# A second copy of x with its columns on partitions in place of the transposes of its rows, norm factors spread by a matrix product, and two alternating units in the first block

## The chip, the core and the metric

The kernel runs on one core of one Trainium2 chip. The metric is the device time of one execution in microseconds (us). A core has TensorE for matrix products (PE in the profile, its weight loads PEld), VectorE (DVE), ScalarE (ACT), GpSimd (POOL) and SyncE (SP), whose queue issues nearly all DMA transfers here. Each engine works through its own instructions in order and waits on the others by semaphores.

## What is computed

One layer of a streaming encoder over 4096 prompt frames and 64 sample frames with a model width of 1024, cut to what the change touches:

```python
def rms_norm(x, w):
    y = x * lax.rsqrt(jnp.mean(x * x, axis=-1, keepdims=True) + EPS)
    return y * w

h = rms_norm(x, norm_in_w) @ w_in          # 1024 -> 5648 columns
u, v, g, z, xbc, dt_raw = jnp.split(h, SPLITS, axis=-1)
# gMLP branch: s = u * (W_s LN(v) + b), times silu(g)
# SSD branch: conv + silu on xBC, scan over chunks with dt, times silu(z)
y = x + concat([a_out, b_out]) @ w_out     # then a last rms_norm
```

All values are float32. A product on TensorE contracts over partitions, so the normalised rows of x are needed with the 1024 columns of x on partitions, not with the frames there.

## The kernel before

**Blocks and stages.** The frames stand in chunks of 128. Five blocks of six chunks (768 frames) are worked through in turn by `Strassen(bi).run()`, and then a last block with two prompt chunks and the 64 sample frames. A block goes through the stages v, conv, u and g, and z; the z stage also builds the operands of the next block. After all blocks a second phase multiplies by w_out.

**Products.** The input projection of a block uses a scheme with seven products in place of eight (`ORDER = 1, 2, 4, 6, 7, 5, 3`). Each operand is split into a rounded part and a rest ("hi" and "lo"), and a product adds hi·hi, hi·lo and lo·hi. The operands that come from x are the tiles `hop[1]` to `hop[7]`, each with hi and lo; in rows of the trace they are all `hop`. They are made from `xq`, the normalised x with columns on partitions (a view of the tile `arena`), by the steps T1 to T4 (line 524, 527, 530, 533) and `split` (cast on ACT, line 514, and a subtraction, line 515). With frames cut in halves h = 0, 1 and columns in halves kh = 0, 1, `xq` has four quarters b11, b12 (kh = 0) and b21, b22 (kh = 1). `hop[1]` needs the quarter b11 alone and `hop[2]` the quarter b21 alone; all the others need the second half of the frames too.

**x before.** For the first block `rows0_load`, `rows0_norm` and `rows0_turn` load each chunk's rows, square and sum them on ACT, raise the mean to -1/2 on POOL (line 123), multiply the rows on DVE (line 612), transpose them on PE (line 619) and copy them out of PSUM with the factor `norm_in_w` (lines 624 and 626). For later blocks `xrows` does the same in the z stage (lines 479, 481, 488, 491), once for each half of the columns, so every chunk is loaded one and a half times.

**Weights.** In the first block the class `Operands` makes the weight operands from `w_in` (`make`): sums of raw tiles a11, a12, a21, a22 (tiles `wx`, `wa`), a cast on ACT (line 392) and a subtraction on DVE or POOL (line 393), and it stores them in DRAM (`wop_v` and others, line 397) for later blocks, which load them again (line 417, 420). A request of unit v takes two tiles `w` of four, so two products of v can be ready at a time, and a tile is free again when its product is done and its store has landed.

**Order of the work.** Filler steps are spread over the products by `fill.tick()`. In the v stage of the first block, `hooks` puts the making of `hop[3]` to `hop[7]` behind the first products of unit v0; unit v1 follows with the same seven operands. A scheduler in the language decides the final order on each engine's queue; the lists below show it.

## Time and profile before

| | |
|---|---|
| median of three runs | 2957.9 us (2953.92 to 2960.72) |
| the profiled execution | 2957.03 us, its span 2955.1 us |
| PE busy | 2826.3 us (96%) |
| DVE busy | 2162.7 us (73%) |
| ACT busy | 1345.8 us (46%) |
| POOL busy | 704.8 us (24%) |
| DMA | 679.14 MB, 230 GB/s in the mean |

The page is read from the top: PE is the busiest engine over the whole span, so a gain has to come from fewer columns streamed on PE, from less waiting of PE, or from a higher granted clock. The queries that follow cut the span by stage.

### The profile page before, as it was taken

What the parts mean: (1) busy time and instruction counts of PE and PEld (TensorE: products, weight loads), DVE (VectorE), ACT (ScalarE), POOL (GpSimd) and SP (SyncE); (2) the same over time, 40 slices, a digit from 0 to 9 for tenths busy, and PEclk for the clock granted to TensorE, in tenths of its full rate; (3) what the DMA queues carried; (4) which work ended last, traced back from release to release, by engine and by line L of the source; (5) the groups of instructions that cost most, each with busy time, mean ns of one, the idle gap of its engine ahead of it and who ended that gap; (6) DMA issues with size and microseconds to landing.
All of it is one profiled execution on the core that took longest, in us unless ns stands there. A gap on an engine that the chain in (4) does not pass through costs nothing. (4 is left out here: it accounts for less than half of the span.)

```text
span 2955.1 us, 46403 instructions
## 1 busy us (share of the span) xinstructions
PE 2826.3 (96%) x17159; PEld 2633.3 (89%) x17159; DVE 2162.7 (73%) x3607; ACT 1345.8 (46%) x2655; POOL 704.8 (24%) x575
## 2 busy tenths in 40 slices
PE   5988988999999999999999999999999899999998
PEld 5987887999999999999999999999899688878886
DVE  7888887667756777676677576874666766698887
ACT  4366655145643266541565514663365222253332
POOL 4554443110012100031000221000301433353332
PEclk8999998999999999999999999999999899999999
DMA  6666777777787777886777877778777555454553
GB/s 223 252 233 237 258 281 261 245 229 238 248 277 270 229 238 243 270 288 227 244 241 240 300 264 229 234 246 281 241 251 226 168 171 171 159 169 157 171 171 111
DMA packets 306809, 679.14 MB, mean 230 GB/s; under 512 B 30472, under 2 KB 154072, under 8 KB 306584
## 3 DMA queue, kind: packets, MB, share of 16 engines
q1 hardware_dynamic: 305544, 676.17, 68.6%
q8 instruction: 137, 2.24, 0.3%
q14 instruction: 88, 0.72, 0.1%
q10 hardware_dynamic: 1040, 0.00, 0.0%
HBM read 525.34 MB, written 150.75 MB: 229 GB/s over the span
## 5 line engine op out<-in xcount | busy, mean ns | idle before, releaser
L1123 PE MATMUL mm<-hop,w 128*128 128x384 f32 x1656 | 579.4, 350 | 7.1 <-ACT w L392 3.5
L1125 PE MATMUL mm<-hop,w 128*128 128x384 f32 x1656 | 564.9, 341 | 9.0 <-DVE w L393 4.5
L1124 PE MATMUL mm<-hop,w 128*128 128x384 f32 x1656 | 565.0, 341 | 0.0
L1629 PE MATMUL pa<-wlo,oh 128*128 128x512 f32 (+1 forms) x928 | 366.7, 395 | 13.0 <-DVE wlo L1583 13.0
L1630 PE MATMUL pa<-whi,ol 128*128 128x512 f32 (+1 forms) x928 | 364.9, 393 | 3.5 <-DVE ol L1591 3.5
L1628 PE MATMUL pa<-whi,oh 128*128 128x512 f32 (+1 forms) x928 | 365.2, 394 | 2.6 <-ACT whi L1582 1.4
L1123 PEld LDWEIGHTS mm<-hop,w 128*128 128x128 f32 x1656 | 315.4, 190 | 14.0 <-ACT w L392 7.0
L1125 PEld LDWEIGHTS mm<-hop,w 128*128 128x128 f32 x1656 | 315.3, 190 | 12.2 <-DVE w L393 7.0
L1124 PEld LDWEIGHTS mm<-hop,w 128*128 128x128 f32 x1656 | 315.5, 190 | 3.4 <-issue 2.4
L1123 PE MATMUL mm<-hop,wy 128*128 128x384 f32 x864 | 297.4, 344 | 0.0
L1125 PE MATMUL mm<-hop,wy 128*128 128x384 f32 x864 | 292.0, 338 | 0.0
L1124 PE MATMUL mm<-hop,wy 128*128 128x384 f32 x864 | 291.9, 338 | 0.0
L1629 PEld LDWEIGHTS pa<-wlo,oh 128*128 128x128 f32 (+1 forms) x928 | 174.6, 188 | 57.1 <-DVE wlo L1583 18.9
L1630 PEld LDWEIGHTS pa<-whi,ol 128*128 128x128 f32 (+1 forms) x928 | 174.8, 188 | 42.7 <-DVE ol L1591 4.2
L1628 PEld LDWEIGHTS pa<-whi,oh 128*128 128x128 f32 (+1 forms) x928 | 174.5, 188 | 42.5 <-ACT whi L1582 2.1
L123 POOL TENSOR_TENSOR rsx<-rsx,mhalf 128x1 f32<-128x1 f32 (+1 forms) x33 | 19.0, 588 | 736.6 <-DVE rsx L122 736.6
L1083 PE MATMUL mm<-w,hop 128*128 128x260 f32 x552 | 160.4, 291 | 16.2 <-ACT hop L514 16.2
L1085 PE MATMUL mm<-w,hop 128*128 128x260 f32 x552 | 159.6, 290 | 7.7 <-DVE hop L515 7.7
L882 ACT ACTIVATE acb<-acb,acu 128x128 f32<-128x128 f32 (+1 forms) x528 | 166.6, 389 | 0.6
L1124 PEld LDWEIGHTS mm<-hop,wy 128*128 128x128 f32 x864 | 162.6, 188 | 0.7
L1123 PEld LDWEIGHTS mm<-hop,wy 128*128 128x128 f32 x864 | 162.5, 188 | 0.8
L1125 PEld LDWEIGHTS mm<-hop,wy 128*128 128x128 f32 x864 | 162.3, 188 | 0.0
(333 smaller groups left out, 6517.8 us busy)
## 6 DMA issues: line engine op xcount, KB each, us to landing
w<-wop_c SPq DMA_DIRECT2D x114, 512.0 KB, 4.3
w<-wop_v SPq DMA_DIRECT2D x84, 520.0 KB, 5.0
w<-wop_u SPq DMA_DIRECT2D x76, 512.0 KB, 4.3
w<-wop_g SPq DMA_DIRECT2D x76, 512.0 KB, 4.4
w<-wop_z SPq DMA_DIRECT2D x76, 512.0 KB, 4.6
wy<-wop_c SPq DMA_DIRECT2D x72, 512.0 KB, 4.4
acb<-acd SPq DMA_DIRECT2D x66, 512.0 KB, 5.1
raw<-ab SPq DMA_DIRECT2D x64, 512.0 KB, 4.1
```

What stands on the lines that cost most here:

```text
L123: pool.tensor_tensor(out, out, mhalf[: out.shape[0]].to_broadcast(list(out.shape)), ALU.pow)
L882: act.activation(M[:L, i, :L], M[:L, i, :L], AF.Relu, bias=self.acu[:L, ci, h0 + i : h0 + i + 1])
L1083: pe.matmul(pv, a, hi[:, j, :], start=(j == 0), stop=False)
L1085: pe.matmul(pv, b, hi[:, j, :], start=False, stop=(j == 3))
L1123: pe.matmul(b, hi[:, j, :], thi[:, j, :], start=j == 0, stop=False)
L1124: pe.matmul(b, hi[:, j, :], tlo[:, j, :], start=False, stop=False)
L1125: pe.matmul(b, lo[:, j, :], thi[:, j, :], start=False, stop=j == 3)
L1628: pe.matmul(b, x[0][:, j, :], hi, start=first, stop=False)
L1629: pe.matmul(b, x[0][:, j, :], lo, start=False, stop=False)
L1630: pe.matmul(b, x[1][:, j, :], hi, start=False, stop=last)
```

## The change

The program gets one more input, `x_t`: the prompt and the sample with columns as rows (1024 x 4160), laid out before the launch. `xload` loads a quarter of it straight into `xq`. The rows of x are still loaded once for each chunk, only for the sum of squares (`norms`, `norms0`), and for later blocks this moves into the conv stage of the block ahead. `spread` multiplies the identity by a chunk's factors and multiplies ones by that on PE, which leaves the factors of 384 frames in PSUM on all partitions; `xscale` multiplies a stretch of `xq` by them and by `norm_in_w` in one DVE instruction. In the first block the products run v0 and v1 for 1, then v0 and v1 for 2, then the rest of v0 and the rest of v1. The raw tile a11 of v1 stands in a spare part of `arena`, and the sums of v's raw tiles move from POOL to DVE (one of four stays). T3 and the subtractions of `hop[5]` and `hop[3]` move from POOL to DVE in the first block.

```diff
+        def v_order(bi):
+            a, b = ([(("v", i), q) for q in ORDER] for i in range(2))
+            if bi:
+                return a + b
+            return [a[0], b[0], a[1], b[1]] + a[2:] + b[2:]
...
-                if q == 1:
+                if q == 1 and not v:
                     eng.tensor_tensor(r["a21"], r["a21"], r["a22"], ADD)
...
+                if v and q == 4:
+                    dve.tensor_tensor(r["a21"], r["a21"], r["a22"], ADD)
+                    dve.tensor_tensor(r["a11"], r["a21"], r["a11"], SUB)
+                    dve.tensor_tensor(r["a22"], r["a22"], r["a11"], SUB)
+                    pool.tensor_tensor(r["a12"], r["a12"], r["a11"], SUB)
...
-                dve.tensor_scalar(t[:L, : D // 2], t[:L, : D // 2], rsx[:L, ci : ci + 1], None, ALU.mult)
-            def turn(ci):
-                for i in range(4):
-                    pe.transpose(pt[:, i, :L], t[:L, i * P : (i + 1) * P], ident[:L, :L])
-                for i in range(4):
-                    act.activation(xq[:, k, off : off + L], pt[:, i, :L], AF.Copy, scale=nwt[:, k : k + 1])
...
+        def spread(chunks):
+            for i in range(0, len(chunks), HC):
+                dg = wk.tile([P, HC, P], F32, tag="xl", name="dg", bufs=1)
+                dve.tensor_tensor(
+                    dg, bc(ident, 1, [P, HC, P]), bc(rsx[:, i : i + HC], 2, [P, HC, P]), ALU.mult
+                )
+                pt = psf()
+                pe.matmul(pt[:, :n], ones, dg.rearrange("p c t -> p (c t)")[:, :n], start=True, stop=True)
+        def xload(chunks, kh, o, n):
+            sp.dma_start(
+                xq_view(T)[:, 4 * kh : 4 * kh + 4, o : o + n],
+                x_t[4 * kh * P : (4 * kh + 4) * P, t0 : t0 + n].rearrange("(k p) t -> p k t", p=P),
+            )
+        def xscale(chunks, k, o, n, r):
+            xk = xq_view(sum(c[1] for c in chunks))[:, k, o : o + n]
+            dve.scalar_tensor_tensor(xk, xk, nwt[:, k : k + 1], r[:, :n], ALU.mult, ALU.mult)
...
-            0: ([lambda ci=ci: rows0_norm(ci) for ci in (3, 4, 5)] + turns0[3], turns0[4]),
-            1: (turns0[5] + ro["T1"] + ro["T2"] + ro["T4"] + ro[4], []),
-            2: (ro[6] + ro["T3"], []),
+            0: ([lambda: norms0(1)] + scale0(1, 0) + scale0(1, 1), []),
+            1: (ro["T1"] + ro["T2"] + ro["T4"] + ro[4], []),
+            2: (ro[6], ro["T3"]),
...
+                fill.later += norms(blocks[bi + 1])
-                fill.later += xrows(nxt, 0, T2)
+                fill.later += columns(nxt, 0, fac)
```

Three places show how the queues change. The first is the start. Before, POOL holds two sums of v's raw tiles (lines 401 and 403) and then the subtractions of `hop3`, T3 (line 530) and those of `hop5`:

```order
L401 TENSOR_TENSOR wx_182<-wx_194,wx_182 128x1040
L403 TENSOR_TENSOR wa12_188<-wa12_188,wx_182 128x1040
L515 TENSOR_TENSOR hop3_154<-arena_155,hop3_154 128x768
L1165 COPY cvr_1192<-carp_145 128x3
L530 TENSOR_TENSOR arena_155<-arena_155 128x2x384
L515 TENSOR_TENSOR hop3_154<-arena_155,hop3_154 128x768
L530 TENSOR_TENSOR arena_155<-arena_155 128x2x384
L515 TENSOR_TENSOR hop5_153<-t1_474,hop5_153 128x768
L515 TENSOR_TENSOR hop5_153<-t1_475,hop5_153 128x768
```

After, the end of the same stretch stands on DVE: T2 (line 560), T4 (566), the subtractions of `hop6` and `hop4` (550), two sums of v0's raw tiles (412, 413), T3 (563), and only then the "lo" of v0's second weight operand (`w_330`, from the raw tile `wa12_197`):

```order
L560 TENSOR_TENSOR arena_155<-arena_155,t1_377 128x2x384
L560 TENSOR_TENSOR arena_155<-arena_155,t1_378 128x2x384
L566 TENSOR_TENSOR arena_155<-arena_155 128x2x384 x2
L550 TENSOR_TENSOR hop6_151<-arena_155,hop6_151 128x768
L550 TENSOR_TENSOR hop4_150<-arena_155,hop4_150 128x768 x2
L550 TENSOR_TENSOR hop6_151<-arena_155,hop6_151 128x768
L412 TENSOR_TENSOR wx_208<-wx_208,wx_205 128x1040
L563 TENSOR_TENSOR arena_155<-arena_155 128x2x384
L413 TENSOR_TENSOR wx_188<-wx_208,wx_188 128x1040
L563 TENSOR_TENSOR arena_155<-arena_155 128x2x384
L550 TENSOR_TENSOR hop7_152<-arena_155,hop7_152 128x768
L404 TENSOR_TENSOR w_330<-wa12_197,w_329 128x1040
```

Ahead of these rows on DVE stand eight scalings (line 526) and the two halves of T1. The work of POOL has moved into the DVE queue, ahead of the weight operand of the third product.

The second place is PE in the z stage of the second block. Before, four transposes of one chunk (line 488) stand between the matmuls of the products, twelve such groups in a full stage:

```order
L1125 MATMUL mm<-hop_148,wy 128x384
L1123 MATMUL mm<-hop_149,w 128x384
L488 MATMUL ss<-ident,xt 128x128 x4
L1124 MATMUL mm<-hop_149,w 128x384
L1125 MATMUL mm<-hop_149,w 128x384
```

After, two single products of ones with the spread factors (line 511) stand in the stage, near its beginning; this is the first:

```order
L1151 MATMUL mm<-hop_149,w 128x384
L1152 MATMUL mm<-hop_149,w 128x384
L511 MATMUL pt<-dg,ones 128x384
L1150 MATMUL mm<-hop_150,w 128x384
L1151 MATMUL mm<-hop_150,w 128x384
```

The transposes are gone from the queue, and nothing else has taken their places.

The third place is DVE at the start of the same z stage. Before, the multiplication of a chunk's rows (line 481) stands between the sums that empty the banks of the products (lines 1138 to 1153):

```order
L1138 TENSOR_TENSOR arena<-mm,arena 128x3x128
L1145 TENSOR_TENSOR arena<-mm,arena 128x3x128
L1147 TENSOR_TENSOR arena<-mm,arena 128x3x128
L1148 TENSOR_TENSOR arena<-mm,arena 128x3x128
L122 TENSOR_SCALAR rsx<-ss_8272 128x1
L1150 TENSOR_TENSOR arena<-mm,arena 128x3x128
L481 TENSOR_SCALAR xt<-xt,rsx 128x512
```

After, eight scalings (line 526), which need the columns that `xload` brings, stand in one piece between the sum of product 2 (line 1165) and that of product 6 (line 1172):

```order
L1239 TENSOR_TENSOR at<-arena,at 128x768 x2
L1165 TENSOR_TENSOR arena<-mm,arena 128x3x128
L507 TENSOR_TENSOR dg<-ident,rsx 128x384
L526 SCALAR_TENSOR_TENSOR arena<-arena,nwt,pt 128x384 x8
L1172 TENSOR_TENSOR arena<-mm,arena 128x3x128
L1174 TENSOR_TENSOR arena<-mm,arena 128x3x128
```

The sums behind them now wait for that load.

## Rows read from the trace of the kernel before

**Rows 1.** The page: span.

```profile
span 2955.1 us, 46403 instructions
```

**Rows 2.** PE waits over the whole span: line, what it waited for, us in total, times, longest.

```profile
PE mm L1083 <- ACT hop L514: 16.2, 2, 15.0
PE ss L488 <- DVE xt L481: 15.3, 14, 4.0
```

**Rows 3.** PE waits from 400 to 530 us alone, same columns.

```profile
PE ss L488 <- DVE xt L481: 7.7, 4, 4.0
...
PE mm L1085 <- DVE hop L515: 2.8, 1, 2.8
```

**Rows 4.** Stretches: length, busy PE, PEld, DVE, ACT, POOL (instructions), PEclk, DMA share, GB/s.

```profile
31.60:46.60 15.00, 0.01 (x1) 0.00 (x0) 8.86 (x15) 7.06 (x12) 12.43 (x7) 0.68 0.17 68
46.60:60.00 13.40, 11.04 (x57) 10.44 (x58) 13.40 (x11) 5.23 (x8) 8.18 (x5) 0.60 0.49 177
463.00:510.00 47.00, 38.68 (x196) 37.23 (x197) 37.92 (x49) 25.54 (x54) 12.27 (x7) 0.87 0.71 264
839.00:908.00 69.00, 65.66 (x386) 63.34 (x385) 35.89 (x58) 34.94 (x82) 13.50 (x10) 1.00 0.91 307
```

**Rows 5.** Timeline of PE, start to end of the first v stage: start, duration.

```profile
9.22 2.31 PE L619 MATMUL ss<-ident,arena 128*128 128x128 f32 x8 [9.22 <-DVE arena L612]
...
15.23 0.57 PE L1083 MATMUL mm<-w,hop 128*128 128x260 f32 x1
15.59 0.42 PE L1084 MATMUL mm<-w,hop 128*128 128x260 f32 x1
15.81 0.42 PE L1083 MATMUL mm<-w,hop 128*128 128x260 f32 x1
...
46.63 0.80 PE L1083 MATMUL mm<-w,hop 128*128 128x260 f32 x2 [15.02 <-ACT hop L514]
...
108.17 0.28 PE L1084 MATMUL pt<-w,hop 128*128 128x260 f32 x1
108.29 0.28 PE L1085 MATMUL pt<-w,hop 128*128 128x260 f32 x1
```

**Rows 6.** Timeline of POOL and DVE in the first v stage.

```profile
34.22 6.45 POOL L515 TENSOR_TENSOR hop<-arena,hop 128x768 fp32r<-128x768 f32 x1 [2.57 <-ACT hop L514]
42.52 1.82 POOL L515 TENSOR_TENSOR hop<-arena,hop 128x768 fp32r<-128x768 f32 x1
...
47.12 5.11 DVE L515 TENSOR_TENSOR hop<-arena,hop 128x768 fp32r<-128x768 f32 x2
56.14 3.54 DVE L515 TENSOR_TENSOR hop<-arena,hop 128x768 fp32r<-128x768 f32 x4
59.60 1.23 DVE L393 TENSOR_TENSOR w<-wx,w 128x1040 fp32r<-128x1040 f32 x1
```

**Rows 7.** DMA from 0 to 60 us in 40 slices of 1.5 us.

```profile
GB/s 0 213 169 350 397 357 391 418 371 300 294 301 294 50 3 24 225 169 391 419 399 402 114 19 0 0 0 0 0 0 158 197 355 327 28 0 0 80 286 334
```

**Rows 8.** Timeline of PE around four transposes in the second block's z stage.

```profile
842.70 0.34 PE L1125 MATMUL mm<-hop,w 128*128 128x384 f32 x1
842.87 0.60 PE L488 MATMUL ss<-ident,xt 128*128 128x128 f32 x4
...
843.49 0.34 PE L1124 MATMUL mm<-hop,w 128*128 128x384 f32 x1
```

**Rows 9.** Timeline of PE around one product of two whole float32 operands, 512 columns.

```profile
253.61 1.02 PE L978 MATMUL pst<-xdt,bt 128*128 128x512 f32 x2
...
254.64 0.34 PE L1124 MATMUL mm<-hop,w 128*128 128x384 f32 x1
```

**Rows 10.** One tile's instructions: duration min/median/max in ns, first and last start.

```profile
L762 DVE SCALAR_TENSOR_TENSOR arena<-ss,prm,bT x80: 468/607/753, 137.4 to 1803.7; 128x512 f32<-128x512 f32 x40, 128x256 f32<-128x256 f32 x40
...
L488 PE MATMUL ss<-ident,xt x216: 222/273/421, 425.0 to 2065.6; 128*128 128x128 f32 x104, 64*128 64x64 f32 x4
```

**Rows 11.** Timeline of DVE where the second block's operands are made (T2).

```profile
512.39 4.92 DVE L527 TENSOR_TENSOR arena<-arena,t 128x768 f32<-128x768 f32 x2 [2.04 <-ACT arena L491]
```

More of the change, by code (lines that the diff above doesn't have):

```diff
@@ L450, in xq_view, with sums_of, norms @@
             return arena[:, : KT * T].rearrange("p (k t) -> p k t", k=KT)
-        def halves(chunks):
-            return [(off, L, gc, smp) for off, L, gc, smp in chunks]
-        def xrows(chunks, kh, T, tag="acb"):
-            xq = xq_view(T)
+        def sums_of(ss, ci, t, L):
+            sq = wk.tile([P, D], mybir.dt.bfloat16, tag="xh", name="sqj", bufs=1)
+            act.activation(sq[:L], t[:L], AF.Square, accum_out=ss[:L, ci : ci + 1])
+        def norms(chunks):
+            n = len(chunks)
@@ new lines, in load, with square @@
+                sp.dma_start(t[:L], x_sample[0] if smp else x_prompt[0, gc * P : gc * P + P, :])
+                held[ci] = t
+            def square(ci):
+                if ci == 0:
+                    held["ss"] = wk.tile([P, SB], F32, tag="ss1", name="ss1")
+                    dve.memset(held["ss"], 0.0)
+                sums_of(held["ss"], ci, held.pop(ci), chunks[ci][1])
+                if ci == n - 1:
+                    rsqrt_mean(rsx[:, :n], held["ss"][:, :n], 1.0 / D)
+            steps = [lambda: load(0)]
@@ L501, in xrows, with columns @@
+        def columns(chunks, kh, fac):
+            T = sum(c[1] for c in chunks)
+            steps = [lambda: xload(chunks, kh, 0, T)]
+            if not kh:
+                steps.append(lambda: fac.extend(spread(chunks)))
+            for k in range(4 * kh, 4 * kh + 4):
+                steps.append(lambda k=k: [xscale(chunks, k, o, n, r) for o, n, r in fac])
             return steps
@@ L688, in mixing_bias @@
                 )
-        for ci in range(3):
+        for ci in range(HC):
             rows0_load(ci)
+        xload(blocks[0], 0, 0, N2)
         ops.fetch(1)
-        for ci in range(3, SB):
+        xload(blocks[0], 1, 0, N2)
+        for ci in range(HC, SB):
             rows0_load(ci)
+        ops.fetch(3)
+        xload(blocks[0], 0, N2, N2)
+        xload(blocks[0], 1, N2, N2)
         ops.fetch()
@@ new lines, in v_stage @@
+                    hi, lo = ops.get(self.bi, ("v", vg), q)
+                    thi, tlo = hop[q][:, 0], hop[q][:, 1]
+                    pvs = []
+                    for i in range(HC):
+                        pv = (pm() if i < 2 else psf())[:, :WGD]
+                        for j in range(4):
+                            a, b = thi[:, j, i * P : (i + 1) * P], tlo[:, j, i * P : (i + 1) * P]
+                            pe.matmul(pv, a, hi[:, j, :], start=(j == 0), stop=False)
+                            pe.matmul(pv, a, lo[:, j, :], start=False, stop=False)
+                            pe.matmul(pv, b, hi[:, j, :], start=False, stop=(j == 3))
+                        pvs.append(pv)
@@ new lines, in v_stage @@
+                    before, after = hooks.pop(iq, ([], []))
+                    run(before)
+                    ops.ahead()
+                    fill.tick()
+                    for i, pv in enumerate(pvs):
+                        c11, c12 = V[:, i, gl], V[:, HC + i, gl]
+                        c21, c22 = V[:, i, gr], V[:, HC + i, gr]
+                        stat = lambda c, g: dve.bn_stats(self.bst[:, c, g, :], V[:, c, g, :WG])
+                        self.add_up(q, pv, (c11, c12, c21, c22))
+                        if q == 2:
+                            stat(i, gl)
+                        elif q == 7:
+                            stat(i, gr)
+                        elif q == 5:
+                            stat(HC + i, gr)
+                        elif q == 3:
+                            stat(HC + i, gl)
@@ L1107, in v_stage @@
+                    run(after)
+                    while pend and q == 5 and vg == 0:
+                        pend.pop()(psf())
                 dve.tensor_tensor(
@@ L1293, in run @@
                 fill.later += self.z_silu(1) + self.z_fin(2, acc) + self.z_fin(3, acc)
[L1294 removed]
+                rows = columns(nxt, 1, fac)
                 if final:
@@ L1297, in run @@
                 else:
-                    fill.later += rows[:4] + ro[1] + rows[4:]
+                    fill.later += rows[:1] + [lambda: None] * 3 + ro[1] + rows[1:]
                     for nm in (2, "T2", "T4", 4, 6):
```

158 lines of the change are left out of this document (53 added, 105 removed).

## The prediction

> **What bounds the kernel now.** I read the page from the top: PE works for 96% of a span of 2955.1 us [rows 1], so the change can only win where PE waits, where it runs at half clock, or where it streams something that isn't needed. The waits of PE come next. Over the whole span two groups belong to the parts that are changed [rows 2]: two waits for `hop`, one of 15.0 us, and fourteen waits of the transposes (line 488), 15.3 us. Half of the latter, 7.7 us, falls between 400 and 530 us, in the z stage of the first block, where the first operand wait behind it costs another 2.8 us [rows 3]. So the transposes of the four later transitions wait 15.3 − 7.7 = 7.6 us together.
>
> The windows show the same places from the side of the engines [rows 4]. From 31.6 to 46.6 us PE does nothing, DVE is busy for 8.86 of 15 us, and POOL for 12.43. The next 13.4 us run at a granted clock of 0.60. In the stretch from 463 to 510 us PE is busy 38.68 of 47 us at 0.87. In a later z stage, 839 to 908 us, PE is busy 65.66 of 69 us at 1.00: there only 3.3 us are to be had from waits, and the rest of the gain has to be columns that are not streamed. DMA is at 0.91 and 307 GB/s there, so this is also where a late load would hurt.
>
> The timeline of PE gives the first v stage [rows 5]: transposes from 9.22, first matmul at 15.23 with a spacing of 0.22 (15.59 to 15.81), the wait until 46.63, and the last two matmuls 0.12 apart (108.17, 108.29). Fourteen products of 36 matmuls at 0.12 are 60.5 us; the stage takes 93.3. Of the 32.8 us between, 15.0 are the wait; from 46.63 on, twelve products need 52 us and take 62, so 10 more go to half clock and small waits.
>
> **A, first v stage.** Its start: 24 transposes and the multiplication of rows go, three squares, one `dg`, one product of ones and four scalings come. The first product starts at about 15 us as before (chain: last of the first rows loaded, square, factor, `dg`, product, scaling, cast), since it needs 1.57 MB of rows, 0.79 MB of columns and 0.53 MB of weights, which the first twelve or so microseconds of the DMA rates bring [rows 7].
>
> Now the wait. Up to 19.5 us the queue moved 5.8 MB before [rows 7]. After, the columns of the second half of the frames stand behind 6.84 MB and are done at 8.41 MB; the rest of 2.6 MB at 300 to 400 GB/s ends at 26 to 28.5 us, its first quarter by about 25. v0 and v1 of operand 1 fill PE from 15 to about 28. The third product then needs its weight's "lo" on DVE, and in the changed queue this stands behind eight scalings, T1 to T4 and five subtractions of `hop` (13 half tiles), and two sums with its own subtraction. Scaling is not in the trace; the nearest row is line 762, one instruction of the same kind on 128x512 or 128x256 from SBUF and PSUM, median 607 ns [rows 10]: I take 0.6, with 0.47 and 0.75 as its ends. Half tiles cost 0.89 us when POOL is quiet (3.54 for four) and 2.56 when it isn't (5.11 for two); the weight's subtraction 1.23 [rows 6]. So 25 + 8×0.6 + 13×0.89 + 3×1.23 = 25 + 4.8 + 11.6 + 3.7 = 45 us. The alternation gives PE a product more of cover, but the operands of the third stand behind work that POOL used to share: the third product starts at 45 rather than 46.6. Then twelve products, 52 us, and what is lost beside: 10 before; I take 7, since the later subtractions cost 0.89 in place of 2.56 with POOL nearly empty. End 104 in place of 108.4: **−4**. Bounds: −11 if the queue is done by 38, +3 if the loads end at 31 or half tiles run at 1.3.
>
> That a half tile costs 0.89 or 2.56 us by POOL's activity is what the rows show (POOL itself takes 6.45 there and 1.82 elsewhere [rows 6]). [...]
>
> The first product meets a PE that has done no transposes. [...]
>
> **B, z stage of the first block (412 to 530).** Twelve groups of four transposes go. One costs PE 843.49 − 842.87 − 0.17 = 0.445 us [rows 8], so 5.34 us go. Two products of ones with whole float32 operands come: 0.86 us at 512 columns (254.64 − 253.61 − 0.17 [rows 9]), 0.64 at 384. Net −4.06. The 7.7 us of transposes that wait [rows 3] go: their chain (load, square, factor, multiply, transpose, copy) is off PE, and the norms are already done in the conv stage. The 2.8 us at the first operands go too, for T2, which took until 517.3 [rows 11], no longer follows transposed columns. That is 14.6; the two scalings of eight, 2×8×0.6 = 9.6 us of DVE in a stretch where it is busy 37.92 of 47 [rows 4], against twelve multiplications and 96 copies that leave DVE and ACT, give back something: **−13**, bounds −4 (all waits come back as waits for the load) and −20 (the clock at 0.87 also rises; 13% of 47 us is 6).
>
> **C, three full transitions (blocks 1 to 4).** Transposes: 3 × −4.06 = −12.2. Waits: of 7.6 us I take half, 3.8, as gained. The reason for half: now eight scalings in one piece stand on DVE between the sums of products 2 and 6, and they wait for a load of 1.57 MB, issued when the last matmuls of the scan are done, which is about where that stretch of 839 to 908 begins. With nothing beside it that is 5.1 us at 307 GB/s; among the weights about 12, so it lands near 851. A product fills a bank with twelve matmuls of 0.17 [rows 8], 2.0 us; after two products and some start-up, near 845, DVE stands before the scalings, 6 us, and scales for 4.8. PE goes on into four banks, 8.2 us of cover, so about 2.6 us of wait are new at each. **−16**, bounds −10 and −22.
>
> **D, last transition.** It has two chunks and the sample: six groups, 6×0.445 less one product of 320 columns, 0.53: **−2**.
>
> **E, conv stages.** Six loads of rows and six squares move there; they replace one and a half loads for each chunk in the z stage. PE needs none of it; ACT is at 46% overall. 0, up to +3 if that cover is short and conv waits for DMA.
>
> Sum: −4 − 13 − 16 − 2 = −35 from the profiled 2957.0, which is 0.9 below the median. That gives **2922 us**.
>
> **Rivals.**
> R1: the alternation covers the start. If DVE's order does not matter, because the third product's weight is done early or half tiles run while loads are awaited, the third product starts at about 34; twelve products with 7 lost end at 93. Then −15 in place of −4, and 2911; with the clock of B restored (its end of −20), 2904. For it: DVE idles before 25 us. Against it: the row order of the changed queue, with the weight last. Chance 0.15.
>
> R2: only the streamed columns are won. The waits come back in another name: DVE at its scalings, the sums behind, the banks. Then B is −4, C −12 + 3×2.6 = −4, D −2, A −2: 2945. For it: DMA at 0.91 and DVE at 37.92 of 47. Against: in 839 to 908 only 3.3 us of wait exist now, and DVE is busy 35.89 of 69. Chance 0.13.
>
> R3, slower: the column load is late at every transition. Behind the scalings stand the sums that empty PE's banks, so each microsecond of landing beyond the cover of 8.2 is one of PE. To eat the 35 us, four transitions must lose some 9 us each on top of what the forecast has there; the load has then to land near 860 instead of 851, 21 us after its issue. It decides if the load gets less than 75 GB/s of the 307. At 863 the time is 2922 + 4×12 = 2970. Against it: the queue before this stage holds only about three row loads and the weights. Chance 0.05.
>
> Within 0.2% (some 6 us, what a measurement here can tell): A at +3 with R2 elsewhere and some loss in the conv stages, 0.04. My forecast keeps 0.63.
>
> **How the numbers follow.** Faster: 0.63 + 0.15 + 0.13 = 0.91; same 0.04; slower 0.05. The range holds the forecast with its bounds (the ends of A, B and C do not all fall on one side), R1 to 2904 and R2 to 2945: 2900 to 2944.
>
> **What would show it.** The changed profile should have no rows of lines 488 and 619; a wait of PE before the third product that ends near 45 us with DVE as its releaser (R1: near 34); the first v stage ending near 104; half tiles of `hop` at 0.89 us in the start; scalings at 0.6; PE busy some 16 us less in total; no wait for `xt`, and at the later z stages a wait for DVE of 1 to 3 us behind the scalings (R3: 9 or more, R2: 2 to 4 and a clock still below 0.9 in the first). I am wrong if the scaling costs well over 0.75 us, if the loads at the start land after 31 us, or if conv stages lengthen by more than 3 us in all.

## The result and the profile after

The changed kernel takes 2925.4 us (median of four runs, 2922.99 to 2929.74), beside 2956.6 us of the kernel before, measured with it (four runs): a ratio of 0.9895, with a 95% interval from 0.9877 to 0.9912. The forecast was 2922 us, with a range from 2900 to 2944. The page after, with the span (against [rows 1]), the busy times, and the packets of the instruction queue q8:

```profile
span 2924.9 us, 45556 instructions
...
PE 2800.6 (96%) x16917; PEld 2607.1 (89%) x16917; DVE 2184.0 (75%) x3613; ACT 1283.8 (44%) x2415; POOL 670.2 (23%) x537
...
q8 instruction: 135, 2.21, 0.3%
```

PE is busy 25.7 us less, DVE 21 us more. The last row plays a part below: 135 packets with 2.21 MB, 16 KB each, for 2×16917 instructions of PE, so one packet for about 250 of them. Before, it is 137 packets with 2.24 MB for 2×17159, the same 250. That these packets carry PE's instructions is read from this ratio, and from runs e9 to e12, where matmuls added on PE move them.

Next, PE's waits after, over the whole span (in total, times, longest); they answer to [rows 2]:

```profile
PE pt L651 <- DVE dg L649: 13.8, 2, 11.3
...
PE ss L956 <- issue: 13.3, 3, 4.7
...
PE mm L1110 <- ACT w L403: 12.2, 1, 12.2
```

The transposes' waits are gone with the transposes. The wait of 15.0 us has become one of 12.2 us for a weight tile, and ahead of it stands another of 11.3 us, at the very start, for the first `dg` (9.2 us before, for the first rows [rows 5]).

**Where the 30 us lie.** The product matmuls are the same 11232 before and after, so each has a start in either trace, and the difference of the two is what was won (−) or lost (+) up to there. A few of them, by number:

| matmul | place | before | after | difference |
|---|---|---|---|---|
| 73 | third product of the first block | 46.6 | 45.0 | −1.6 |
| 505 | first of conv | 108.4 | 103.8 | −4.6 |
| 1153 | u and g, first block | 276.0 | 275.0 | −0.9 |
| 1441 | u and g, later | 353.9 | 360.1 | +6.1 |
| 1729 | z, first block | 430.0 | 436.8 | +6.8 |
| 2161 | v, second block | 534.1 | 521.9 | −12.1 |
| 9793 | u and g, fifth block | 2019.1 | 1991.8 | −27.4 |
| 11232 | the last one | 2281.0 | 2250.9 | −30.0 |

Set beside the terms of the sum, the first v stage, forecast −4, gave −4.6. The three full transitions with the blocks around them (2161 to 9793), forecast −16, gave −15.2. The last transition and block, forecast −2, gave −2.7. Two terms were off, and they offset each other: conv, u and g of the first block, forecast 0 to +3, lost 11.4; the z stage of the first block, forecast −13, gave −18.9.

**The start after,** PE's timeline (start, duration), which answers to [rows 5]:

```profile
11.35 1.65 PE L651 MATMUL pt<-dg,ones 128*128 128x384 f32 x2 [11.35 <-DVE dg L649]
15.09 0.80 PE L1110 MATMUL mm<-w,hop 128*128 128x260 f32 x2 [2.10 <-ACT hop L549]
...
26.02 1.49 PE L651 MATMUL pt<-dg,ones 128*128 128x384 f32 x2 [2.41 <-DVE dg L649]
...
45.00 0.80 PE L1110 MATMUL mm<-w,hop 128*128 128x260 f32 x2 [12.16 <-ACT w L403]
...
47.22 0.59 PE L1111 MATMUL mm<-w,hop 128*128 128x260 f32 x1 [1.20 <-DVE w L404]
```

and DVE's, from the first scaling of the second half of the frames to the "lo" of the third product, against [rows 6]:

```profile
27.56 2.19 DVE L526 SCALAR_TENSOR_TENSOR arena<-arena,nwt,pt 128x384 f32<-128x384 f32 x4 [0.44 <-PE pt L651]
...
38.41 2.70 DVE L550 TENSOR_TENSOR hop<-arena,hop 128x768 fp32r<-128x768 f32 x3 [0.48 <-ACT hop L549]
...
44.19 0.95 DVE L563 TENSOR_TENSOR arena<-arena 128x768 f32<-128x768 f32 x1
45.06 0.95 DVE L550 TENSOR_TENSOR hop<-arena,hop 128x768 fp32r<-128x768 f32 x1
45.93 1.24 DVE L404 TENSOR_TENSOR w<-wa,w 128x1040 fp32r<-128x1040 f32 x1
```

The reader is to see that DVE hardly pauses from 27.56 to 47.2, that four scalings take 2.19 us and three half tiles 2.70, and that the weight of the third product is the last in this row, as the order of the queue had it. What ends PE's wait is the cast on ACT, whose queue stands behind T3 of DVE as well (a cast of `hop` released by line 563 at 43.16, the cast of the weight at 43.90).

**A later z stage after.** DVE at the scalings of the second block's z stage:

```profile
831.44 0.56 DVE L507 TENSOR_TENSOR dg<-ident,rsx 128x384 f32<-128x384 f32 x1
831.91 4.33 DVE L526 SCALAR_TENSOR_TENSOR arena<-arena,nwt,pt 128x384 f32<-128x384 f32 x8
836.51 0.56 DVE L1172 TENSOR_TENSOR arena<-mm,arena 128x384 f32<-128x384 f32 x1 [0.27 <-PE mm L1152]
```

At this first half of the columns DVE doesn't wait for them, and the sum behind the scalings waits for PE, not PE for it: the 2.6 us of new waits that the forecast had for the banks didn't come here. Half as much came at the second half of the columns. DVE stands for them and then scales, the sums that empty the banks (line 1174) come late, and PE waits for two of them:

```profile
877.11 4.29 DVE L526 SCALAR_TENSOR_TENSOR arena<-arena,nwt,pt 128x384 f32<-128x384 f32 x8 [2.15 <-DMA arena<-in_x_t_dram]
...
884.53 0.44 PE L1150 MATMUL mm<-hop,w 128*128 128x384 f32 x1 [0.44 <-DVE arena L1174]
...
887.78 0.45 PE L1150 MATMUL mm<-hop,wy 128*128 128x384 f32 x1 [0.87 <-DVE arena L1174]
```

PE's waits in that stage, 815 to 905 us, are these and one for a weight tile; the next two full transitions have the same:

```profile
PE mm L1150 <- DVE arena L1174: 1.3, 2, 0.9
PE pt L1111 <- DMA wy<-wop_v: 0.7, 1, 0.7
```

**Busy and idle time of PE.** A stretch can also be split into what PE was busy and what it stood. These are the windows of the first z stage, from matmul 1729 to 2161, and of the three full transitions, 2161 to 9793, before and after in turn (columns as in [rows 4]):

```profile
429.99:534.07 104.08, 84.74 (x475) 81.37 (x474) 76.72 (x100) 54.73 (x114) 37.31 (x24) 0.89 0.73 258
...
436.79:521.93 85.14, 73.89 (x434) 71.37 (x433) 71.21 (x94) 36.92 (x59) 31.54 (x19) 0.94 0.78 284
```

```profile
534.07:2019.14 1485.07, 1475.14 (x9858) 1440.53 (x9857) 1050.50 (x1870) 703.15 (x1427) 154.65 (x175) 1.00 0.76 251
...
521.93:1991.79 1469.86, 1463.22 (x9725) 1429.08 (x9723) 1071.25 (x1884) 668.13 (x1286) 157.00 (x161) 1.00 0.78 257
```

In the first, PE is busy 10.9 us less and stands 8.1 us less; in the second, 11.9 and 3.3.

### The profile page after: what moved, and what is told of

The parts are those of the page before. It is cut to its first block, busy times and chain, and to the rows that moved or that the text cites. A ratio compares the mean times of both kernels' runs of the same rounds, so it can differ in the third digit from the quotient of the medians.

```text
span 2924.9 us, 45556 instructions
## 1 busy us (share of the span) xinstructions
PE 2800.6 (96%) x16917; PEld 2607.1 (89%) x16917; DVE 2184.0 (75%) x3613; ACT 1283.8 (44%) x2415; POOL 670.2 (23%) x537
## 3 DMA queue, kind: packets, MB, share of 16 engines
q8 instruction: 135, 2.21, 0.3%
## 5 line engine op out<-in xcount | busy, mean ns | idle before, releaser
L1150 PE MATMUL mm<-hop,w 128*128 128x384 f32 x1656 | 577.8, 349 | 14.9 <-ACT w L403 6.9
L1110 PE MATMUL mm<-w,hop 128*128 128x260 f32 x552 | 160.4, 292 | 14.4 <-ACT w L403 12.2
L1202 ACT ACTIVATE arena<-cvr,prm 128x768 f32<-128x768 f32 x60 | 61.5, 1027 | 192.6 <-DVE cvr L1177 152.9
```

What stands on the lines that cost most here:

```text
L1110: pe.matmul(pv, a, hi[:, j, :], start=(j == 0), stop=False)
L1150: pe.matmul(b, hi[:, j, :], thi[:, j, :], start=j == 0, stop=False)
L1202: act.activation(o, raw[:, 3 : 3 + TS], AF.Identity, bias=prm[:, CB + c : CB + c + 1], scale=cw(3))
```

## The experiments

Three things were open: what sets the third product, what the 11.4 us in the first block's conv, u and g are, and how the transposes' own time and their waits share the gain. This table has for every run the time won (−) or lost (+) against the trace of before, stretch by stretch, from the starts of the matmuls of the table above (the numbers at the head). "To 505" is the first v stage, "2161" the first z stage, "9793" the three full transitions.

| run | median, us | to 505 | to 1153 | to 1441 | to 1729 | to 2161 | to 9793 | to 11232 |
|---|---|---|---|---|---|---|---|---|
| changed kernel | 2925.4 | −4.6 | +3.7 | +7.1 | +0.7 | −18.9 | −15.2 | −2.7 |
| e1 units in turn | 2932.3 | +0.4 | +1.8 | +6.0 | +0.7 | −17.8 | −14.4 | −0.9 |
| e2 POOL again | 2939.5 | +4.9 | +1.2 | +6.8 | +0.6 | −18.1 | −14.9 | +1.0 |
| e3 stores first | 2924.2 | −5.6 | −0.1 | +4.7 | +1.2 | −18.2 | −14.6 | −0.7 |
| e4 norms in z | 2936.5 | −3.4 | +0.4 | +5.7 | −0.7 | −6.9 | −15.9 | −2.6 |
| e5 first block only | 2958.0 | −4.6 | −0.9 | +8.3 | +0.3 | +0.2 | −3.9 | +1.0 |
| e6 idle transposes | 2934.1 | −4.6 | +1.8 | +5.3 | +1.2 | −19.2 | −7.7 | +1.3 |
| e7 load thrice | 2944.6 | −3.9 | +1.2 | +5.9 | +0.4 | −14.6 | −5.4 | 0.0 |
| e8 before, one input more | 2950.1 | −0.4 | −2.1 | +1.2 | −3.0 | −2.2 | −0.4 | +0.7 |
| e9 128 products | 2932.3 | −1.2 | +2.6 | +7.0 | +0.8 | −18.8 | −16.1 | +2.2 |
| e10 50 products | 2924.7 | −4.4 | 0.0 | +2.1 | +0.7 | −19.0 | −12.1 | +1.6 |
| e11 stores first, 50 | 2922.5 | −4.0 | −0.8 | +2.0 | +1.3 | −19.0 | −13.2 | +5.1 |
| e12 before, 75 products | 2966.7 | +4.6 | +0.3 | +5.9 | −0.3 | 0.0 | 0.0 | +1.5 |

e8 is the kernel before in all that it executes, so its row says how much of a number here is the difference of two executions: up to 3 us in a stretch, in this one pair. e5, whose later blocks have the code of before, shows −3.9 over the three transitions.

**e1: the alternation undone.**

```diff
-            if bi:
-                return a + b
-            return [a[0], b[0], a[1], b[1]] + a[2:] + b[2:]
+            return a + b
```

> The changed kernel with one part undone: in the first block all seven products of unit v0 come before those of v1, as before the change. Theory 1 (the third product waits for DVE's and ACT's queues and for a weight tile that is free when its store has landed, and these don't depend on the unit): the third product starts at 45 us +-2, the time is that of the changed kernel, 2925 +-4. Rival (the alternation is what covers the wait): the third product starts 5 us or more later, the time is 2930 to 2937.

The ratio to before is 0.9909 (0.9896 to 0.9921). The third product starts at 45.1, as theory 1 said, but the time is the rival's. PE's waits of the first v stage tell why:

```profile
PE mm L1108 <- ACT w L401: 11.2, 1, 11.2
PE mm L1109 <- DVE w L402: 6.1, 2, 5.8
```

The third product is now product 4 of v0, and 5.8 us go at the "lo" of its weight (line 402), where the changed kernel waits 1.2. With the alternation, the third product needs only `hop[2]`, long done, and v1's behind it as well; that DVE's making of the later `hop` tiles is therefore less in the way is argued, not tried. The alternation is worth 5 us in the v stage, behind the wait, not by covering it.

**e2: POOL works beside DVE again.**

```diff
-                    dve.tensor_tensor(lo[:, s], src(s), hi[:, s].bitcast(F32), SUB)
+                    (pool if start and q in (5, 3) else dve).tensor_tensor(
+                        lo[:, s], src(s), hi[:, s].bitcast(F32), SUB
+                    )
...
-                dve.tensor_tensor(b12[:, sl[i]], b22[:, sl[i]], b12[:, sl[i]], SUB)
+                (pool if start else dve).tensor_tensor(b12[:, sl[i]], b22[:, sl[i]], b12[:, sl[i]], SUB)
```

> The changed kernel, with T3 and the subtractions of hop5 and hop3 of the first block back on POOL. Theory 1 (POOL beside DVE makes half tiles cost 2.5 us in place of 0.9): half tiles of hop in the first 60 us are over 1.5 us again, the third product starts at 48 us or later, the v stage ends 4 to 10 us later, the time is 2929 to 2935. Rival (sharing the work relieves DVE): the v stage ends earlier, and the first conv stage, which lost 4 us, gains; the time is 2917 to 2923.

The ratio is 0.9934 (0.9922 to 0.9946), the v stage ends 9.5 us later than in the changed kernel. DVE's half tiles there:

```profile
43.63 7.24 DVE L550 TENSOR_TENSOR hop<-arena,hop 128x768 fp32r<-128x768 f32 x4 [6.51 <-ACT hop L549]
51.95 0.94 DVE L550 TENSOR_TENSOR hop<-arena,hop 128x768 fp32r<-128x768 f32 x1
```

Four take 7.24 us, 1.8 each, where three took 2.70 above. Theory 1 holds on the half tiles and the stage; the third product starts at 47.7, just short of its 48, and the time is 4 us above its range. But the dearer half tiles are only 3.6 us of DVE's time. The first of them also stands behind 6.5 us of idle DVE: the casts on ACT that it needs come after one that waits until 40.57 for T3 on POOL, where a subtraction ahead of T3 took 4.74 us. Together the move off POOL is worth more than the other parts of the changed start that were undone.

**e3: the first weight stores ahead of the parameter loads.**

```diff
         ops.fetch()
-        parameters()
...
         run(scale0(0, 1) + ro[2])
         ops.ahead(1)
+        parameters()
```

> The changed kernel, with the loads of the small parameters put behind the first weight stores in SP's queue, so that the weight tiles of the first product come free about 8 us earlier; the weight operand of the third product then also stands further ahead on DVE. Theory 1 (that wait was set by the store, 34.5 us at issue, and then the queues): the third product starts at 33 to 38 us, the v stage ends 7 to 12 us earlier, and if nothing is given back the time is 2914 to 2918. Rival (the first conv stage is bound by DVE and POOL, which make the weight operands, and gives the gain back): the v stage ends earlier, but from the third conv product on the time stands as in the changed kernel, 2921 to 2926.

The ratio is 0.9883 (0.9870 to 0.9896), not to be told from the changed kernel's. The third product starts at 37.8, so the place of the store had set that; with it the order on ACT moved, where the cast of this weight now starts at 36.65, ahead of the casts that wait for T3, in place of 43.90. But the v stage ends only 1 us earlier, not 7 to 12, and in between DVE is full:

```profile
38.00:60.00 22.00, 18.06 (x113) 17.34 (x114) 21.91 (x30) 7.33 (x11) 3.64 (x2) 0.79 0.69 245
```

DVE is busy 21.91 of 22 us (the third of the pairs). Six of the seven microseconds won at the third product go before the stage ends, so it isn't conv that takes them: the rival was right on the time and wrong on the place.

**e4: the second block's norms in the first block's z stage.**

```diff
-                fill.later += norms(blocks[bi + 1])
+                if bi:
+                    fill.later += norms(blocks[bi + 1])
...
+                if not bi:
+                    fill.later += norms(nxt)
                 fill.later += columns(nxt, 0, fac)
```

> The changed kernel, with the row loads and squares for the second block moved from the first block's conv stage to its z stage. In the profile of the changed kernel the first block lost 12 us between the end of v and the start of z. Theory 1 (the loss is of the queues of DVE and POOL and of a late weight load, not of these loads): the first block's conv, u and g stages stay as long, the time is 2925 +-3. Rival (the six loads and squares in the conv stage cause it): these stages are 5 to 12 us shorter, the time is 2914 to 2920, unless the z stage then waits for the factors.

The ratio is 0.9930 (0.9918 to 0.9942). Theory 1 holds for the stages, not for the time: conv gains some 3 us against the changed kernel's trace, 1 against the other traces with the same code up to there (e6 and e7), and u and g lose what they lost. And the z stage wins 6.9 us in place of 18.9: 12 of these hang on the norms being ready. (Here all six norms are late together, while before the change each chunk's came with its own rows, so 12 us is the price of this order and not exactly what the old one lost.)

**e5: only the first block as changed.** In the later blocks the old `xrows` stands again, and there are no `norms`.

```diff
-                fill.later += norms(blocks[bi + 1])
...
-                fill.later += columns(nxt, 0, fac)
+                fill.later += xrows(nxt, 0, T2)
...
-                rows = columns(nxt, 1, fac)
+                rows = xrows(nxt, 1, T2)
```

> The first block as changed, but for the later blocks the rows are loaded, multiplied and transposed in the z stage as before the change, and no row loads or squares stand in the conv stages. Theory 1 (the changed start is worth 4 to 5 us and what the first block gives back in conv, u and g comes with the start, whatever stands in conv): the third product starts at 45 us, 5 us are ahead at the end of the v stage, 0 to 4 us behind at 430 us, no gain at the transitions; the time is 2957 +-4. Rival (what is given back is due to the row loads and squares in conv): the 5 us stay, the time is 2953 or less.

The ratio is 1.0007 (0.9997 to 1.0017): the changed start alone is worth nothing here, as theory 1 had it. It wins 4.6 us and loses 8.3 between matmuls 1153 and 1441, without a row load or square in conv; what that loss is, is told below. In sum, the kernel's gain is made from the first z stage on.

**e6: as many transposes as before, of the identity.**

```diff
+            def turns():
+                pt = ps4()
+                for i in range(4):
+                    pe.transpose(pt[:, i, :], ident, ident)
+
+            return steps + [turns] * len(chunks)
```

> The changed kernel with as many transposes as before the change put back into the z stages, of the identity into a PSUM bank that nobody reads: 12 groups of four at each of four transitions and 6 at the last. They wait for no data. Theory 1 (a group costs PE 0.445 us of its own time): 54 x 0.445 = 24 us more than the changed kernel, 2949 +-4. Rival (transposes fill time in which PE waits anyway, and the gain came from the waits alone): under 10 us more, 2926 to 2935.

The ratio is 0.9933 (0.9914 to 0.9953). They are all there, and each takes what it took [rows 8, 10]:

```profile
L540 PE MATMUL ss<-ident x216: 270/272/273, 439.9 to 2042.5; 128*128 128x128 f32 x108
```

They cost 8.7 us, not 24, as the rival had it: nothing in the first z stage (−19.2 beside −18.9) and 7.5 at three transitions, where 36 × 0.445 would be 16. The window of that z stage says where the rest is, to be read beside the waits of the changed kernel there:

```profile
815.00:905.00 90.00, 90.00 (x571) 88.74 (x570) 59.34 (x89) 34.48 (x53) 16.97 (x10) 1.00 0.86 307
```

PE is busy all of 90.00 us; in the changed kernel it is busy 87.96. The transposes fill 2 us in which PE otherwise waits. Over the three transitions PE's idle time falls from 6.6 to 1.0 us. The rest of their time does lengthen these stages, so the rival is right on the sum and not in all of its reason. (They wait for no data, so this is the price of the columns alone, at the places where the idle groups stand.)

**e7: the columns three times.**

```diff
-            steps = [lambda: xload(chunks, kh, 0, T)]
+            steps = [lambda: [xload(chunks, kh, 0, T) for _ in range(1 if kh else 3)]]
```

> The changed kernel, with the load of the columns of the first half at each of five transitions made three times over into the same tile, so that it lands some 12 to 14 us later, near 838 us in the second block. Theory 1 (banks cover about 4 us more after product 6, then PE stands with DVE): 2 to 5 us at each of the transitions, the time is 2933 to 2948. Rival (the loads wait for nobody, DVE has time to spare): under 1 us each, 2925 to 2929. Third possibility (each microsecond of lateness is one of PE, as the rival forecast of a slower kernel has it): 10 us or more each, 2965 or more.

The ratio is 0.9964 (0.9951 to 0.9977), 19 us more than the changed kernel, within theory 1's range, but not by its mechanism. The scalings of the second block's z stage, with DVE's idle time in brackets where there was any:

```profile
848.30 0.56 DVE L1165 TENSOR_TENSOR arena<-mm,arena 128x384 f32<-128x384 f32 x1 [1.36 <-PE mm L1152]
848.77 4.28 DVE L526 SCALAR_TENSOR_TENSOR arena<-arena,nwt,pt 128x384 f32<-128x384 f32 x8
```

They stand 17 us later, behind a later sum in DVE's order, and PE has no wait for a bank at all. What it pays comes afterwards, PE's waits from 880 to 1200 us (0.2 us and none in the changed kernel):

```profile
PE pt L1070 <- POOL ssum L1266: 2.5, 1, 2.5
PE mm L1110 <- ACT arena L1163: 1.5, 1, 1.5
```

So part of a late load is paid by the last norm of the block and its neighbours; by the table it costs 3 to 4 us a transition. That the banks would make DVE's wait PE's own, as the slower rival had it, wasn't tried, since the order moved with the load.

**e8: the kernel before with one input more.** `x_t` is declared and not read; the program is otherwise that of before.

> The kernel before, with the new input x_t declared but never read. Theory 1 (the loss of 4 to 6 us between 275 and 345 us in every version of the changed kernel has its cause in the change's instructions or their timing): the profile shows that stretch as in the profile of before, PE's wait for the first scan product near 285 us is 1.8 us, the time is that of before, 2957 +-4. Rival (it comes from where tensors lie in memory with one more input, or varies from run to run): that wait is over 4 us and 4 us are lost by 345 us.

One execution, 2950.1 us, which is below the expected range and within the spread of the kernel before in the same series (2945.9 to 2961.1, 19 runs). PE's wait near 285 us is 2.0 us, and 1.2 are lost by matmul 1441: theory 1. So the input alone doesn't make the loss there. That chance doesn't either, one execution can't show; the fourteen traces below do.

**The loss near 285 us.** In every version of the changed kernel so far, 4.7 to 8.3 us were lost between matmuls 1153 and 1441. The traces of before and after have the same instructions there in the same order on SP, ACT, DVE and POOL; the difference begins with two loads of raw weight tiles. The DMA rows of the stretch 271 to 276 us of before (issues, KB, us from issue to landing):

```profile
wx<-in_w_in_dram SPq DMA_DIRECT2D x2, 512.0 KB, 5.6
```

and of 270 to 276 us after:

```profile
q8 instruction: 1, 0.02, 1.0%
...
wx<-in_w_in_dram SPq DMA_DIRECT2D x2, 512.0 KB, 7.0
```

After, a packet of PE's instructions falls into these loads. The time to landing in the rows is that of the second (7.0 us in place of 5.6); the trace doesn't tell that of the first. ACT's cast waits for the first, which was issued at 271.11 us before and at 270.19 after, so it starts 4.7 us after the issue before and 6.4 after. Before and after, in one fence each:

```profile
275.80 0.62 ACT L392 CAST w<-wx 128x512 fp32r<-128x512 f32 x1 [0.18 <-DMA wx<-in_w_in_dram]
```

```profile
276.57 0.62 ACT L403 CAST w<-wx 128x512 fp32r<-128x512 f32 x1 [1.85 <-DMA wx<-in_w_in_dram]
```

Behind it in the queues of ACT and DVE stand the operands of the scan's next product (line 956), and PE waits 4.39 us for them (1.82 before). PE's rows name "issue", but the last operand, `acb` on DVE, ends 0.1 us ahead of PE's start both times; before and after:

```profile
284.04 1.45 DVE L890 TENSOR_TENSOR acb<-acb,cbm 128x1024 f32<-128x1024 f32 x1
...
285.59 1.09 PE L928 MATMUL ss<-acb,xdt 128*64 128x128 f32 x16 [1.82 <-issue]
```

```profile
285.62 1.52 DVE L918 TENSOR_TENSOR acb<-acb,cbm 128x1024 f32<-128x1024 f32 x1
...
287.24 1.98 PE L956 MATMUL ss<-acb,xdt 128*64 128x128 f32 x16 [4.39 <-issue]
```

From 285 to 305 us PE's granted clock is 0.83, where it was 1.00 before; much of the rest of the loss is there. The change took instructions from PE ahead of this place: the 48 transposes of the start went, each with its weight load, and two products of ones came, in two passes each (x2 in the rows of line 651). That is 96 − 8 = 88 instructions fewer, and the packets moved: between 262 and 276 us the one of before lies at 267 to 268, the one of after at 274 to 275. The last four runs test that. Each adds matmuls of 128 columns, whose results nobody reads, in PE's wait ahead of the third product (here 50 of them):

```diff
+                    if self.bi == 0 and iq == 1:
+                        pv = pm()[:, :P]
+                        for j in range(50):
+                            pe.matmul(pv, thi[:, j % 4, :P], hi[:, j % 4, :P], start=True, stop=True)
```

**e9: 128 of them, a whole packet.**

> The changed kernel with 128 matmuls of 128 columns between the second and third product of the first block, where PE waits for 12 us; nobody reads what they make. They are 256 instructions of PE with their weight loads, 16 KB of code, as much as one packet of the queue that brings PE's instructions (q8). Theory 1 (the loss near 285 us comes from such a packet that falls into the load of a weight tile, and its place follows from the count of PE's instructions): with a whole packet more its place is that of the changed kernel, the wait near 285 us stays at 4 us or more. On the clock: if PE kept busy starts the third product at full clock, the v stage ends 3 to 6 us earlier, at 98 to 101 us; the rival is that DVE sets the pace of the products behind the wait, and the stage ends at 103 to 104. Time 2921 to 2926.

The packet falls into the load again (the cast starts 6.6 us after the issue), the wait is 4.4 us and 7.0 us are lost: as theory 1 said. The ratio is 0.9925 (0.9908 to 0.9943), 7 us more than the changed kernel and above the expected range, for both expectations on the v stage failed: it ends 3.4 us later than in the changed kernel. The third product ran at a granted clock of 1.00 (windows of it, in this kernel and in the changed one):

```profile
45.30:50.40 5.10, 4.66 (x38) 4.46 (x38) 5.10 (x7) 1.06 (x1) 4.27 (x1) 1.00 0.67 264
```

```profile
45.00:52.60 7.60, 6.40 (x37) 6.10 (x38) 7.60 (x8) 1.79 (x2) 5.35 (x2) 0.66 0.70 280
```

5.1 us in place of 7.6, at 1.00 in place of 0.66, after a PE that was busy for all of 33 to 45 us (12.00 of 12 us, 0.00 in the changed kernel). Of the 2.5 us, 1.7 are busy time (4.66 in place of 6.40) and the rest is a shorter wait for the "lo" (0.44 in place of 1.20). But behind it PE waited 3.8 us for the "lo" of the next weight. The added matmuls read v1's first weight tile and so keep it until 45 us, which may be why DVE's queue has that "lo" later; this wasn't tried. What the clock would be worth alone is not shown.

**e10: 50 of them, what the change took away.**

> The same with 50 such matmuls, 100 instructions of PE, which is about what the change took away from PE ahead of this place. Theory 1: the packet of PE's instructions moves about 8 us earlier, as it was before the change, the wait near 285 us is under 2.5 us, and 4 to 7 us are won between 275 and 345 us; the time is 2917 to 2921. Rival (the loss has another cause): the wait stays over 4 us, the time is that of the changed kernel, 2925 +-3.

PE's waits from 275 to 305 us:

```profile
PE ss L956 <- issue: 3.2, 1, 3.2
```

No packet falls into the load (the cast starts 4.7 us after the issue, 4.8 in e11), 2.1 us are lost to matmul 1441 in place of 7.1, and the clock stays at 1.00. The wait itself shrinks less than I had said. By matmul 2161 this trace is 8.4 us ahead of the changed kernel's. But the ratio is 0.9897 (0.9882 to 0.9913), the same, and above the expected time: the transitions and the last block give 3 and 4 us back. Whether packets fall differently there too, and cost this, wasn't tried.

**e11: e3 and e10 together.**

> The kernel with the stores ahead of the parameters, together with the 50 matmuls in the wait ahead of the third product. If both effects stand by themselves: the wait near 285 us under 2.5 us, the time 2914 to 2920, the fastest of all. If the start is given back by DVE and the place of PE's instruction packets decides nothing: 2922 to 2926.

The wait is 1.9 us and 2.0 us are lost, but the ratio is 0.9885 (0.9867 to 0.9902). Its lower median, 2922.5, is within the measurement's uncertainty of the changed kernel's and not in the 2914 to 2920 of two effects that stand by themselves; 5.1 us are lost from matmul 9793 on.

**e12: the kernel before, with 75 of them.** The change took 88 instructions from PE, and a packet holds about 250, so some 160 more put a packet about where 88 fewer do; these are 150.

> The kernel before, with 75 matmuls of 128 columns that nobody reads in PE's wait ahead of the third product, 150 instructions of PE. Theory 1 (the place of PE's instruction packets decides the loss near 285 us): a packet now falls into the weight load near 275 us as it does in the changed kernel; PE's wait for the first scan product behind it grows from 1.8 to over 4 us and 4 to 6 us are lost between 275 and 345 us, the time is 2957 to 2963. Rival (it is something else in the change): the wait stays under 2.2 us and the time is that of before, or a little less where the products behind the wait run at full clock, 2952 to 2957.

The ratio is 1.0026 (1.0016 to 1.0037). DMA rows of 276 to 282 us, and PE's waits from 275 to 305 us:

```profile
q8 instruction: 1, 0.02, 1.1%
...
wx<-in_w_in_dram SPq DMA_DIRECT2D x2, 512.0 KB, 7.0
```

```profile
PE ss L928 <- issue: 4.2, 1, 4.2
```

The kernel before now has the loss, 5.9 us between matmuls 1153 and 1441, with none of the change in it. Another 4.6 us go in the v stage, where e9's matmuls cost time too, which puts the time above the expected range.

**All fourteen traces together.** In the four without the loss (before, e8, e10, e11) no packet of PE's instructions starts between the issue of the first of the two loads and ACT's cast, and the cast starts 4.7 to 4.8 us after the issue. In the other ten one does, and the cast starts 5.9 to 7.1 us after it. How a packet whose own transfer takes 0.9 to 1.4 us holds up the load by one to two microseconds, the traces don't tell.

## Why the prediction was right, and where not

The total came out 3 us from the forecast, and that is in part luck: E was missed by some 8 us beyond its range, and B brought 6 us more than its term.

**A, first v stage.** Right in size, in mechanism only in part. The queue of DVE was worked out well: 19.6 us from the first scaling to the "lo" of the third product, forecast 20.1, with half tiles at 0.9 us and scalings at 0.55 (a median of 0.607 with their overlap). But it began at 27.56 and not at 25, and waited then for the factors (line 651) and not for the columns; and what released PE was the cast on ACT, not DVE, whose "lo" ended at 47.2. That these two come to 45.0 is luck. Nor does the start of the third product decide the stage: with the stores first it is at 37.8, and the stage ends 1 us earlier, since DVE is full (e3). That half tiles are cheap beside a quiet POOL and dear beside a busy one is shown: 0.9 us each in the changed kernel, where POOL has nothing from 25.5 to 47.2 us, and 1.8 each in e2 from 43.6 to 50.9, where POOL works nearly throughout. With the wait for POOL's own slow work beside it that is 9.5 us in all. Why POOL's work makes them dear, no run shows. The first product, with no transposes ahead of it, ran at a spacing of 0.22 (18.11 to 18.33), as before, and ahead of the third product PE waited 12.16 us: that the transposes are gone shows no price here.

**B, first z stage.** The term was mis-sized, −13 beside −18.9, and split wrongly. The 4.06 us of streamed columns are worth nothing here: put back, transposes leave the stage as long (e6). The 7.7 and 2.8 us of waits did go, and 4.2 us for `hop` and `wy` with them. But 1.6 us were to be given back, and 7.3 were: 3.4 us more at the casts of the weights (line 403) and 3.9 for a sum (line 1178); PE stood 8.1 us less in all. What the term left out is the other 10.9 us, PE's busy time. Beyond the transposes some 6.8 of that goes with the granted clock, 0.94 in place of 0.89, which the forecast had only in its bound of −20. The clock isn't a gain by itself, though: in e8 the kernel before had 0.95 there, and its stage was 2.2 us shorter, with 2 us more of waits. By experiment, 12 us of the 18.9 hang on the norms being ready (e4); the other 7 are not divided further.

**C, three transitions.** Right in size (−16, −15.2), and by the windows in both halves: PE is busy 11.9 us less, forecast 12.2, and stands 3.3 us less, forecast 3.8. The reason for taking only half of the waits holds in part: DVE did stand before scalings and PE then for the banks, but at the second half of the columns and for 1.3 us at each transition, forecast 2.6. What doesn't hold is that the transposes alone are worth 12.2: put back without data to wait for, they cost 7.5 us, since they fill such waits (e6).

**D** gave −2.7 for −2, with the block behind it; other versions with the same code there gave up to +5.1.

PE's busy time fell by 25.7 us and not by some 16. The 16 had neither the 48 transposes of the start, 8.9 us before against 3.1 for the two products of ones, nor the 6.8 us of B.

**E, conv, u and g of the first block.** This is the step that failed: "0, up to +3 if that cover is short". The row loads and squares did fit it: from matmul 505 to 1153 the versions with them lose −0.8 to 3.7 us, those without (e4, e5) 0.4 and −0.9, which the difference of two executions nearly covers. The rest, 5 to 8 us between 276 and 354 us, has nothing to do with what is computed, and no term of the sum allowed for it. A packet of PE's instructions falls into a weight load, shown from both sides: taken out by e10 and e11, left in by e9, put into the kernel before by e12. Its cost falls on another transfer, for which ACT waits first (1.85 us in place of 0.18) and PE in the end (4.39 in place of 1.82).

**The rivals.** R1 did not come: the alternation doesn't cover the wait (e1). R2, waits under another name, came in the first z stage, with 7.3 us, which didn't keep it from winning more than forecast; in each later one it is the 1.3 us for the banks. R3 wasn't met; with the scalings 17 us later (e7) the price was 3 to 4 us a transition.

What stays open is why the last block varies by 8 us between versions that have the same code there (the last column of the table).

## What to carry to other kernels

Work taken from a busy engine is worth what the engine then does with the time, which putting idle work of the same length back measures at once: here 24 us of transposes were worth 9 of the 31 us won. POOL, put to work beside DVE where DVE sets the pace, cost 9.5 us here and relieved nothing. And a gain of a few microseconds at one place says little in a kernel with tight loads: here 88 instructions fewer on PE in the first 31 us went with a packet of its code in a weight load at 274 us and with 7.1 us lost there; with 50 matmuls put in their place (e10) it was 2.1. Compare the same instruction's start along the trace, not only the ends.

## What the hardware did that was not expected

With one packet of 16 KB of PE's instructions in a 512 KB load, the cast of that tile started 5.9 to 7.1 us after the load's issue, without one after 4.7 to 4.8, and PE's wait behind it was 4.1 to 4.4 us in place of 1.8 to 3.2. Where the packet fell into the load, 4.7 to 8.3 us were lost in the stretch of 78 us, where not, 0 to 2.1; a part of that by the clock after the wait (0.83 in place of 1.00 over 20 us in the changed kernel). PE ran a product at a granted clock of 1.00 when it had been kept busy for 12.00 of 12 us ahead of it (36 matmuls in 5.1 us, 4.66 of them busy), and at 0.66 when it had stood for those 12 us (7.6 us, 6.40 of them busy).
